# Transfers on POOL's queue tied to an ACT instruction instead of a POOL copy, and fewer of them per step

## The chip, the cores and the metric

The kernel runs on one core of a Trainium2 chip. TensorE (PE) multiplies matrices, VectorE (DVE), ScalarE (ACT) and GpSimd (POOL) work on elements, and SyncE (SP) issues most loads. Each engine takes its instructions from its own queue in order; 16 DMA engines move the data of all queues. The metric is the time of one execution on the device in microseconds (us), the median of the runs shown.

## The reference, cut to what matters

One layer of a hybrid trunk on 512 tokens of width 1024, all in float32:

```
h  = RMSNorm(x);  xa, ga, q, k, v, f, gA, gB = h @ W_in
A  = gelu(ga) * RG_LRU(conv4(xa))         # width 1280, 10 tiles of 128 channels
B  = forgetting_attention(q, k, v, f)     # 16 heads of 64
m  = sigmoid(gA) * (A @ P_A) + sigmoid(gB) * (B @ P_B)
x  = x + RMSNorm(m @ W_out)
u  = conv3(RMSNorm(x) @ W_up);  y = (gelu(u_gate) * u_val) @ W_down
out = x + RMSNorm(y)
```

The last product, by W_down (3072 x 1024), is done with seven half-sized products instead of eight. For that the kernel needs sums of quarters of W_down; four of the seven left factors are such sums.

## The kernel before, in words

**Precision.** Every weight block is split into a rounded part `wh` and the rest `wl`, and each product is three matmuls. A block is 128 partitions by 1024 numbers (512 KB). `Split` loads it on SP (L199); `hi` rounds it on ACT (L205) and `lo` subtracts on DVE (L208). `unit(name)` fetches two blocks ahead of the one that it hands out, so the rounding of a block runs two units before its use.

**Stages, in the order of the trace.** The norm of x with the first four blocks, written out by hand under a manual schedule (L607 to L722); `xa` units t = 4 to 9 (one projection each, L751), with which the gates of tile t - 4 go (`gate_mm`, `gate_act`); four `v` units for tiles t = 10 to 13; four more `v1` units with the decays (`batch`, `inflow`, L809 on); ten `ga` units with scans and output gates (L819 on); sixteen half units of `pa` (L905 on); merge gates; attention, eight pairs of heads (L1128 on); then out, up and down.

**What the gates pass on.** `conv_a(t)` (ACT at L543, DVE at L546) writes `xc[t]`; the pool has six such buffers, so that `conv_a(t)` waits until `xc[t-6]` is no longer read. `gate_act(t)` makes `ix[t]` on ACT (L600) and multiplies it by `xc[t]` on POOL (L601), its last reader. `inflow(t)` takes `ix[t]` on DVE (L790), and the scan (L794) and the output gate (L801, L805) follow.

**The sums of W_down.** `down_sums` yields 48 transfers from DRAM to DRAM, all issued by POOL, each 512 KB: 24 copies (`put`, L160) into tiles `td[0..3][0..5]`, and 24 that add to such a tile (`add`, L163). They come in rounds: in round m four copies, then the additions of rounds m - 1, m - 2 and m - 3. An addition needs the tile that an earlier one wrote. POOL's transfers use eight completion counters in turn, so the ninth waits until the first has landed. The tiles are first read late in the kernel, by the loads of the down product.

**How the transfers get their place.** `background(n, w)` traces a copy of one column of the block `w` on POOL (`tick`, L182), which needs the rounded block, and then n transfers under `tc.issue_after` of that copy. `tc.issue_after(i)` puts the instructions that its block traces on i's own engine behind i in that engine's queue; it adds nothing to instructions of other engines, and it does not wait for i to end. `background` is called once in each of nine `xa`/`v` units (L757), once in each `v1` unit (L813), with two transfers in each `ga` unit (L824) and once in each `pa` half unit (L914).

**Who orders a queue.** Outside the manual regions a planner orders each engine's queue before the program runs. Whenever the engine is free in its plan, it gives it the ready instruction that was traced first; an instruction is ready when everything that it depends on is done in the plan. In a manual region the engine's instructions keep their order among themselves, but instructions traced elsewhere may be put between them. In the plan a transfer of 512 KB holds the queue that issues it for one and the same stretch, copy or addition, a little longer than a load of that size takes alone, whatever goes on in other queues.

Of the kernel before, what the change touches and what calls it, by code (L numbers as in the profile page):

```python
# [8 lines left out]
F32 = mybir.dt.float32  # L9
# [7 lines left out]
P = 128  # L17
# [80 lines left out]
def kernel(  # L98
# [16 lines left out]
    act, dve, pool, pe = nc.scalar, nc.vector, nc.gpsimd, nc.tensor  # L115

    cpool = ctx.enter_context(tc.tile_pool(name="consts", bufs=1))
# [5 lines left out]
    def bank(name):  # L123
        return pspools[-1].tile([P, 512], F32, tag="ps", name=name)
# [32 lines left out]
    def down_sums():  # L157

        def put(t, m, src):
            return lambda: nc.gpsimd.dma_start(td[t][m], src)  # L160

        def add(t, m, src):
            return lambda: nc.gpsimd.dma_start(td[t][m], src, accum_op=ALU.add, max_dma_last_dim=D)  # L163

        for m in range(NS + 3):
            if m < NS:
                for t, (i, c) in enumerate(((0, 0), (1, 1), (0, 1), (1, 0))):
                    yield put(t, m, down_block(i, c, m))
            if 0 <= m - 1 < NS:
                yield add(0, m - 1, down_block(0, 1, m - 1))  # L170
                yield add(2, m - 1, down_block(1, 1, m - 1))
            if 0 <= m - 2 < NS:
                yield add(1, m - 2, td[0][m - 2])
            if 0 <= m - 3 < NS:
                yield add(3, m - 3, td[1][m - 3])

    transfers = down_sums()
    tick = cpool.tile([P, 1], F32, name="tick")

    def background(n, w):  # L180

        i = pool.tensor_copy(out=tick, in_=w[0].bitcast(F32)[:, 0, 0:1])  # L182
        with tc.issue_after(i.ins):
            for _ in range(n):
                next(transfers, lambda: None)()

    class Split:
# [14 lines left out]
            return a if len(self.shape) == 1 else a.rearrange("p (a b) -> p a b", a=self.shape[0])  # L202

        def hi(self):
            act.copy(self.wh, self.raw)  # L205

        def lo(self, engine):
            engine.tensor_tensor(out=self.wl, in0=self.raw, in1=self.wh.bitcast(F32), op=ALU.subtract)  # L208
# [35 lines left out]
    def unit(name, ahead=2):  # L244

        i = where[name]
        fetch(i + ahead)
        return ready.pop(name)
# [6 lines left out]
    def project(dst, unit, ah, al, lo=0, hi=S):  # L255
        wh, wl = unit
        for k in range(KD):
            mm3(dst[:, lo:hi], wh[:, k], wl[:, k], turns(ah[:, k, lo:hi]), turns(al[:, k, lo:hi]), k == 0, k == KD - 1)
# [71 lines left out]
    def v_start(c):  # L330
        for p in range(4 * c, 4 * c + 4):
            vt[p] = vpools[c].tile([P, NT, 4, HD], F32R, tag="vy", name=f"v{p}")
        return [bank(f"v{c}_{t}") for t in range(NT)]
# [197 lines left out]
    with ExitStack() as rg:  # L531
        rt, ixt, tt = {}, {}, {}
        last_act = [None]
        with ExitStack() as r0:
# [22 lines left out]
            def gate_prep(t):  # L557
                n = HROWS[t]
                raw = gwpool.tile([P, 4, P], F32, tag="graw", name=f"graw{t}")
                gh = gwpool.tile([P, 4, P], F32R, tag="gh", name=f"gh{t}")  # L560
                gl = gwpool.tile([P, 4, P], F32R, tag="gl", name=f"gl{t}")
                nc.sync.dma_start(raw, rgw[:, t])
                act.copy(gh, raw)
                stacked = 3 * n <= P
                hw = slice(0, 2 if stacked else 4)
                dve.tensor_tensor(out=gl[:, hw], in0=raw[:, hw], in1=gh[:, hw].bitcast(F32), op=ALU.subtract)
                th = gwpool.tile([P, S], F32R, tag="halo_h", name=f"halo_h{t}")
                tl = None
                if stacked:
                    q = slice(2 * n, 3 * n)  # L570
                    dve.tensor_tensor(out=gh[q, 2:4], in0=raw[q, 2:4], in1=gh[q, 2:4].bitcast(F32), op=ALU.subtract)
                    dsts = ((th, 0, xh), (th, n, xl), (th, 2 * n, xh))
                else:
                    tl = gwpool.tile([P, S], F32R, tag="halo_l", name=f"halo_l{t}", bufs=1)
                    dsts = ((th, 0, xh), (tl, 0, xl))
                for dst, o, src in dsts:
                    for c0, c1 in HALO[t]:
                        i = c0 // P
                        nc.sync.dma_start(dst[o : o + c1 - c0].bitcast(F32), src[i][c0 - i * P : c1 - i * P].bitcast(F32))
                        o += c1 - c0  # L580
                gw[t] = gh, gl, th, tl
# [163 lines left out]
            for t in range(NF, TR + NF):  # L745
                u = unit(order[t][0])
                if t - 3 < TR:
                    gate_prep(t - 3)
                if t < TR:
                    ps = bank(f"xa{t}")  # L750
                    project(ps, u, hh, hl)  # L751
                else:
                    if t == TR:
                        pv = v_start(0)
                    v_mm(t - TR, pv, u)
                if t > NF:
                    background(1, u)  # L757
                pgs = gate_mm(t - NF)
                ga = gate_act(t - NF, pgs)
                if t < TR:  # L760
                    conv_a(t, ps)
                    next(ga)
                    split_a(t)
                else:
                    next(ga)
                next(ga, None)
# [7 lines left out]
        def batch(ops):  # L774
            with tc.issue_after(last_act[0].ins):
                for op in ops:
                    last_act[0] = op()
# [32 lines left out]
        for u in range(4):  # L810
            w = unit(f"v1_{u}")
            v_mm(u, pv, w)
            background(1, w)  # L813
            for t in range(5 * u // 2, 5 * (u + 1) // 2):
                batch([rg_tanh(t), rg_exp(t)])
                inflow(t)
# [3 lines left out]
        for t in range(TR):  # L820
            gas[t] = bank(f"ga{t}")
            w = unit(f"ga{t}")
            project(gas[t], w, hh, hl)
            background(2, w)  # L824
            sq, sc = steps.get(t, ((), ()))
            batch([rg_sqrt(i) for i in sq])
            for i in sc:
                scan(i)
            for i in outs.get(t, ()):
                gate_out(i)  # L830
# [76 lines left out]
        for step, (e, half) in enumerate(PA_ORDER):  # L907
            if half == 0:
                pps[e] = bank(f"pa{e}")
            wh, wl = unit(f"pa{e}_{half}", min(2, len(PA_ORDER) - step))  # L910
            for i in range(5):
                k = 5 * half + i
                mm3(pps[e], wh[:, i], wl[:, i], turns(yh[k], SH), turns(yl[k], SH), k == 0, k == TR - 1)
            background(1, (wh, wl))  # L914
            if half == 1:
                act.copy(pa[:, e], pps[e])
            early_sums(step)
# [28 lines left out]
    def prep_alloc(p):  # L946
        bias = []
        for h in (2 * p, 2 * p + 1):
            B = bpool.tile([P, PO[NT]], F32, tag="B", name=f"B{h}")
            nc.gpsimd.dma_start(B, cnd[h : h + 1, :].partition_broadcast(P))  # L950
            bias.append(B)
        for B in bias:
            for b in (3, 2, 1, 0):
                diag = B[:, PO[b + 1] - P : PO[b + 1]]
                pool.tensor_tensor(out=diag, in0=diag, in1=mask, op=ALU.add)  # L955
        return bias

    pq, pk = held("q0", 1), held("k0", 0)
    with ExitStack() as g2:
# [15 lines left out]
        p, n = gp[0], gp[1]  # L975
# [39 lines left out]
    with ExitStack() as at:  # L1015
# [111 lines left out]
        for p in range(KD):  # L1127
            if p == 0:  # L1128
                pq = held("q1", 1)
            now = scores(p, q, k, bias)  # L1130
            if p < KD - 1:
                bias = prep_alloc(p + 1)
            if 0 < p < KD - 1:
                pq = bank(f"q{p + 1}")
                project(pq, (unit if p > 1 else behind)(f"q{p + 1}"), hh, hl)
            elif p:
                pb_part(0, range(KD - 2))
            if prev is not None:
                pts = pt(p - 1, prev)
            if p < KD - 1:  # L1140
                pk = bank(f"k{p + 1}")
                project(pk, behind(f"k{p + 1}", 2 if p else 0), hh, hl)
                q, k = halves(pq, f"q{p + 1}"), halves(pk, f"k{p + 1}")
            else:
                pb_part(1, range(KD - 3))
            if p == 0:
                b.product(4, b.a[:, Y])
                gate_epilogue(b, "a", 0)
                gate_epilogue(b, "a", 1)
            if prev is not None:  # L1150
                av(p - 1, pts)
            if p == KD - 1:
                pb_part(1, range(KD - 3, KD - 2))
            normalise(now)
            prev = now
        pts = pt(KD - 1, prev)
        i = KD - 2
# [246 lines left out]
    p, n = pairs[NU], pairs[NU + 1]  # L1404
# [381 lines left out]
```

## Time and profile before

| | |
|---|---|
| median of the runs shown (884.02 to 884.9) | 884.7 us |
| the profiled execution | 884.92 us, span 883.1 us |
| PE busy | 868.6 us, 98% of the span |
| DVE, ACT, POOL busy | 743.5, 608.4, 236.3 us |
| DMA, mean over the span | 210 GB/s |

A row of a group names line, engine, operation, what is written from what, the count, then busy us and mean ns, and after the bar the idle time before it and what ended it. A row of a timeline begins with its start and its duration. A row of a DMA queue gives packets, MB, and the time of its packets as a share of 16 engines' time in the window. The row `GB/s` gives the rate in 40 equal slices of the window.

### The profile page before, as it was taken

The numbers are of one execution on the slowest core, as the hardware profiler recorded it, in microseconds if no ns is written. First come the engines' busy times: TensorE is split into PE (matmuls) and PEld (weight loads), VectorE is DVE, ScalarE is ACT, GpSimd is POOL, SyncE is SP. The second block draws the span as 40 slices with busy tenths as digits, with TensorE's granted clock in tenths as the row PEclk, the third lists the DMA queues.
The fourth block names the chain that finished last, engine by engine and source line by source line (L and its number), as shares of the span: only waits on it lengthen the run. The fifth ranks groups of instructions, "written<-read, shape, count | busy, mean of one in ns | idle before, by whom it ended". The sixth has DMA issues, their size and how long they took to land.

```text
span 883.1 us, 15782 instructions
## 1 busy us (share of the span) xinstructions
PE 868.6 (98%) x5856; PEld 792.3 (90%) x5856; DVE 743.5 (84%) x1209; ACT 608.4 (69%) x1031; POOL 236.3 (27%) x283
## 2 busy tenths in 40 slices
PE   9999999999999999999999999999999999999996
PEld 7888888888899998888888889999999999888884
DVE  8986479637978849998868599999999999889997
ACT  7565695532466648776754597888888888688774
POOL 4244344535411024232205100242332332100000
PEclk9999999999999999999999999999999999999999
DMA  7787689999865477453506762879899898699864
GB/s 269 242 288 207 188 214 265 227 273 196 190 148 165 120 261 274 133 173 127 203 26 203 234 200 95 192 178 241 210 222 240 209 233 210 230 384 303 280 192 147
DMA packets 71040, 185.24 MB, mean 210 GB/s; under 512 B 7153, under 2 KB 27681, under 8 KB 70578
## 3 DMA queue, kind: packets, MB, share of 16 engines
q1 hardware_dynamic: 47360, 127.72, 43.4%
q0 software_dynamic: 23456, 56.37, 29.8%
q8 instruction: 46, 0.75, 0.3%
q14 instruction: 32, 0.26, 0.1%
q10 hardware_dynamic: 146, 0.14, 0.0%
HBM read 150.69 MB, written 35.73 MB: 211 GB/s over the span
## 4 chain that ended last, share of the span: by engine, by line
PE 83%; DVE 8%; issue 4%; ACT 2%; POOL 2%; DMA 1%; DVEq 0%; ACTq 0%; POOLq 0%
PE up L464 7%; PE up L462 7%; PE up L461 7%; PE dn L1490 2%; PE dn L1488 2%; PE dn L1489 2%; PE ga L252 2%; PE ga L251 2%; PE ga L253 2%; DVE al L357 2%; PE pb L251 2%; PE xa L251 2%; PE v L341 2%; PE xa L253 2%; PE v L342 2%
## 5 line engine op out<-in xcount | busy, mean ns | idle before, releaser
L397 POOL DMA_DIRECT2D ml<-raw_up x42 | 36.1, 859 | 147.6 <-ACT ml L396 82.5
L1360 DVE SCALAR_TENSOR_TENSOR u<-up,cpt,u 128x511 f32<-128x511 f32 x96 | 71.3, 745 | 3.5 <-ACT u L1354 1.8
L1490 PE MATMUL dn<-wh_dn,al 128*128 128x512 f32 (+1 forms) x180 | 66.6, 370 | 1.3 <-DVE al L357 0.7
L1489 PE MATMUL dn<-wl_dn,ah 128*128 128x512 f32 (+1 forms) x180 | 66.1, 367 | 0.5 <-DVE wl_dn L208 0.5
L1488 PE MATMUL dn<-wh_dn,ah 128*128 128x512 f32 (+1 forms) x180 | 65.8, 366 | 0.2 <-ACT ah L1454 0.2
L461 PE MATMUL up<-sh,th 128*128 128x256 f32 x252 | 59.5, 275 | 0.0
L462 PE MATMUL up<-sl,th 128*128 128x256 f32 x252 | 59.5, 275 | 0.0
L208 DVE TENSOR_TENSOR wl_dn<-raw_dn,wh_dn 128x1024 fp32r<-128x1024 f32 x42 | 52.9, 1259 | 5.4 <-ACT wh_dn L205 5.2
L357 DVE TENSOR_TENSOR tl<-t,th 128x1024 fp32r<-128x1024 f32 x42 | 51.1, 1218 | 0.0
L1354 ACT ACTIVATE u<-up,cpt 128x512 f32<-128x512 f32 x48 | 37.0, 778 | 20.1 <-PE up L464 10.0
L205 ACT CAST wh_dn<-raw_dn 128x1024 fp32r<-128x1024 f32 x42 | 44.4, 1058 | 6.1 <-PE dn L1490 3.7
L461 PEld LDWEIGHTS up<-sh,th 128*128 128x128 f32 x252 | 48.4, 192 | 0.0
L462 PEld LDWEIGHTS up<-sl,th 128*128 128x128 f32 x252 | 48.4, 192 | 0.0
L1368 POOL TENSOR_TENSOR yf<-u,u 128x512 f32<-128x512 f32 x23 | 30.5, 1328 | 59.3 <-issue 46.5
L443 ACT CAST th<-t 128x1024 fp32r<-128x1024 f32 x42 | 43.8, 1044 | 2.4
L1490 PEld LDWEIGHTS dn<-wh_dn,al 128*128 128x128 f32 x180 | 34.1, 189 | 8.0 <-DVE al L357 4.1
L955 POOL TENSOR_TENSOR B<-B,mask 128x128 f32<-128x128 f32 x64 | 30.6, 506 | 34.8 <-DMA B<-cnd 33.7
L461 PE MATMUL up<-h2h,mh 128*128 128x256 f32 x168 | 39.7, 275 | 0.0
L462 PE MATMUL up<-h2l,mh 128*128 128x256 f32 x168 | 39.7, 275 | 0.0
L1489 PEld LDWEIGHTS dn<-wl_dn,ah 128*128 128x128 f32 x180 | 34.1, 189 | 5.8 <-DVE wl_dn L208 1.8
L1050 ACT ACTIVATE P<-P,mx 128x384 f32<-128x384 f32 (+3 forms) x64 | 35.2, 552 | 5.3 <-DVE mx L1045 4.3
L464 PE MATMUL up<-sh,tl 128*128 128x256 f32 x252 | 38.4, 275 | 0.0
(731 smaller groups left out, 3252.4 us busy)
## 6 DMA issues: line engine op xcount, KB each, us to landing
raw_up<-in_w_up_dram SPq DMA_DIRECT2D x48, 512.0 KB, 5.5
td<-in_w_down_dram POOLq DMA_DIRECT2D x36, 512.0 KB, 6.3
raw_dn<-td SPq DMA_DIRECT2D x24, 512.0 KB, 5.4
ml<-raw_up POOLq DMA_DIRECT2D x21, 512.0 KB, 5.4
B<-cnd POOLq DMA_DIRECT2D x16, 640.0 KB, 5.7
raw_dn<-in_w_down_dram SPq DMA_DIRECT2D x18, 512.0 KB, 4.4
raw_wo<-in_w_out_dram SPq DMA_DIRECT2D x16, 512.0 KB, 4.4
td<-td POOLq DMA_DIRECT2D x12, 512.0 KB, 11.2
```

The costliest lines, as they stand in the source:

```text
L205: act.copy(self.wh, self.raw)
L208: engine.tensor_tensor(out=self.wl, in0=self.raw, in1=self.wh.bitcast(F32), op=ALU.subtract)
L251: pe.matmul(dst, ah, bh, start=first, stop=False)
L357: dve.tensor_tensor(out=out, in0=a, in1=b, op=ALU.subtract)
L443: act.copy(self.th[i], self.t[i])
L461: pe.matmul(dst, wh[:, k], turns(ah[:, k]), start=first and k == 0, stop=False, skip_group_check=True)
L462: pe.matmul(dst, wh[:, k], turns(al[:, k]), start=False, stop=False, skip_group_check=True)
L464: pe.matmul(dst, wl[:, k], turns(ah[:, k]), start=False, stop=k == KH - 1, skip_group_check=True)
L1360: dve.scalar_tensor_tensor(out=c[:, s:], in0=ps[:, : S - s], scalar=col(C_CFW + 3 * e + j), in1=c[:, s:], op0=ALU.mult, op1=ALU.add)
L1488: pe.matmul(d[:, x], ah[:, k, tok], bh, start=first, stop=False, skip_group_check=True)
L1489: pe.matmul(d[:, x], ah[:, k, tok], bl, start=False, stop=False, skip_group_check=True)
L1490: pe.matmul(d[:, x], al[:, k, tok], bh, start=False, stop=last, skip_group_check=True)
```

## The change

The `tick` copy is gone. `hi` keeps the last rounding that it traced on ACT in `last_hi`, and `background(n)` traces its transfers under `tc.issue_after` of that ACT instruction. In each `ga` unit one transfer is traced instead of two, in `pa` one in every second half unit, and three at each of the eight pairs of the attention, behind `prep_alloc`. So 31 of the 48 are traced up to the end of `pa`, and the other 17 in the attention.

```
     transfers = down_sums()
-    tick = cpool.tile([P, 1], F32, name="tick")
-    def background(n, w):
-        i = pool.tensor_copy(out=tick, in_=w[0].bitcast(F32)[:, 0, 0:1])
-        with tc.issue_after(i.ins):
+    last_hi = [None]
+    def background(n):
+        with tc.issue_after(last_hi[0].ins):
             for _ in range(n):
                 next(transfers, lambda: None)()
...
         def hi(self):
-            act.copy(self.wh, self.raw)
+            last_hi[0] = act.copy(self.wh, self.raw)
...
                 if t > NF:
-                    background(1, u)
+                    background(1)
...
             v_mm(u, pv, w)
-            background(1, w)
+            background(1)
...
             project(gas[t], w, hh, hl)
-            background(2, w)
+            background(1)
...
-            background(1, (wh, wl))
+            if step % 2:
+                background(1)
...
             if p < KD - 1:
                 bias = prep_alloc(p + 1)
+            background(3)
```

## The prediction

> **What bounds the kernel now.** I read the page first: span, engines, chain.
>
> ```profile
> span 883.1 us, 15782 instructions
> PE 868.6 (98%) x5856; PEld 792.3 (90%) x5856; DVE 743.5 (84%) x1209; ACT 608.4 (69%) x1031; POOL 236.3 (27%) x283
> PE 83%; DVE 8%; issue 4%; ACT 2%; POOL 2%; DMA 1%; DVEq 0%; ACTq 0%; POOLq 0%
> ```
>
> PE sets the time: all its idle time is 14.5 us. So little can be won, and whatever makes PE wait is lost in full. From 24 to 260 us, where the transfers run, the waits of PE are these two:
>
> ```profile
> PE ma L461 <- DVE ma L480: 1.5, 1, 1.5
> PE q L253 <- DVE wl_q L208: 0.9, 1, 0.9
> ```
>
> POOL's groups next: what is removed, what is moved, and what stands beside them.
>
> ```profile
> L182 POOL COPY tick<-wh_pa 128x1 f32<-128x1 f32 x16 | 25.1, 1570 | 24.8 <-ACT wh_pa L205 24.8
> L160 POOL DMA_DIRECT2D td<-in_w_down_dram x24 | 13.3, 556 | 0.5 <-issue 0.5
> L163 POOL DMA_DIRECT2D td<-in_w_down_dram x12 | 12.9, 1180 | 0.0
> L163 POOL DMA_DIRECT2D td<-td x12 | 12.6, 1113 | 10.2 <-DMA td<-td 10.2
> ```
>
> The `tick` copies wait for ACT, and the transfers hardly wait for anything of their own: the tick is what holds them back. The timeline of POOL shows how its queue is ordered.
>
> ```profile
> 11.40 2.39 POOL L208 TENSOR_TENSOR wl_xa<-raw_xa,wh_xa 128x1024 fp32r<-128x1024 f32 x1 [0.76 <-ACT wh_xa L205]
> 19.18 4.75 POOL L208 TENSOR_TENSOR wl_xa<-raw_xa,wh_xa 128x1024 fp32r<-128x1024 f32 x2 [5.39 <-ACT wh_xa L205]
> 24.17 0.18 POOL L182 COPY tick<-wh_xa 128x1 f32<-128x1 f32 x1 [0.24 <-ACT wh_xa L205]
> 24.29 0.72 POOL L160 DMA_DIRECT2D td<-in_w_down_dram  x1
> ...
> 40.10 1.35 POOL L182 COPY tick<-wh_xa 128x1 f32<-128x1 f32 x1
> 40.54 1.32 POOL L160 DMA_DIRECT2D td<-in_w_down_dram  x1
> 46.35 1.28 POOL L601 TENSOR_TENSOR ix<-ix,xc 128x512 f32<-128x512 f32 x1 [4.50 <-ACT ix L600]
> ```
>
> The first ix (L601) is traced in unit t = 4, the transfers before it in units 5 to 8. So the queue is not in the order of the trace: what is ready goes ahead of what is older and not ready.
>
> **The change, part by part.**
>
> 1. *The tie.* The new anchor is an instruction of ACT, the transfers are instructions of POOL, and `issue_after` orders only what is on the anchor's own engine. I therefore expect that no transfer is tied to anything: neither to the rounding nor to its place in `ga`, `pa` or the attention. The copies read an input and write fresh tiles, so the first is ready at the start, and the order above says that they go out whenever POOL's queue is free. That the tie holds in some other way is a rival.
>
> 2. *The ticks removed.* 39 POOL copies (the row above has 16 of them). POOL is 27% busy and nothing on PE's waits names them: 0 us.
>
> 3. *Where the transfers go.* Up to 11 us the rest of POOL's start-up work is ahead. One copy fits before the subtraction at 11.40, some five between it and the one at 19.18, and all others follow from 24 us. By then the first loads have landed, so the start costs about 0 (end: if copies went out from 3 us, they would share the engines with the 4.3 MB of first loads; six copies of 1.5 us, see 4, make up to 9 us). After 24 us the planner books one stretch per transfer, a little over a load's 1.3 us, and puts the older ix in between when ready. The ix are some 7 us apart (10 of them from 46.4 to 107.4 below), so four to five transfers stand between two. Counting from six at 24 us: about 20 before the first ix, 33 before ix of t = 3, 47 before t = 6, and all 48 before t = 7, 8 and 9. Ends: one or two per gap, as today (no effect), and all 48 before the first ix, which I exclude because an older ready ix goes first.
>
> 4. *What they cost on the chip.* The DMA queues in three windows: 0 to 60 us (q0 is POOL's; six copies in it), the rates from 0 to 30 us (loads alone), and 218 to 233 us (additions and loads, the engines full).
>
> ```profile
> q0 software_dynamic: 186, 3.15, 15.0%
> GB/s 0 0 66 289 404 421 388 415 415 415 415 426 415 426 404 415 377 383 377 98 246 360 322 336 101 0 0 0 0 0 169 306 224 126 344 754 175 33 142 350
> q0 software_dynamic: 2072, 2.06, 87.4%
> q1 hardware_dynamic: 614, 1.61, 29.9%
> ```
>
> A copy: 15.0% of 60 us / 6 = 1.5 us of all engines. Loads: 415 GB/s. An addition: in 15 us the loads' 1.61 MB take 3.9 us, which leaves 11.1 us for 2.06 MB, or 3.9 additions of 0.524 MB: 2.8 us each. The planner's equal stretch for both is thus too short for an addition, and it does not count the loads at all. POOL issues a transfer only when the eighth before it has landed, or when the tile that it adds to is there; what stands behind it on POOL waits too. For a full engine set from 2 us on:
>
> - ix of t = 3 stands behind the 33rd transfer, which waits for the 25th: 17 copies and 8 additions, 25.5 + 22.4 = 48 us. Loads until then: some 15 MB (of 19.94 up to 120 us) = 36 us. 2 + 48 + 36 = 86, so this ix ends at about 88 us.
> - The last three ix stand behind the 48th, which waits for the 46th: 24 x 1.5 + 22 x 2.8 = 97.6 us. Loads: 22.96 MB up to 157 us, 55 us, less some that a stalled PE asks for later: 53. 2 + 97.6 + 53 = 152.6; three ix of 1.27 us behind it end at about 155.5 us.
>
> ```profile
> q1 hardware_dynamic: 7584, 19.94, 51.3%
> q1 hardware_dynamic: 8590, 22.96, 44.5%
> L601 POOL TENSOR_TENSOR ix<-ix,xc x10: 1265/1273/1652, 46.4 to 107.4; 128x512 f32<-128x512 f32 x10
> L790 DVE SCALAR_TENSOR_TENSOR ix<-r,ix x10: 684/692/694, 109.9 to 125.3; 128x512 f32<-128x512 f32 x10
> L543 ACT ACTIVATE xc<-xa,cpt x10: 762/777/822, 21.5 to 75.6; 128x512 f32<-128x512 f32 x10
> ```
>
> One rule of the Trainium skill prices this differently: DMA: Bandwidth & Descriptors, "Anatomy of one DMA — SWDGE (gpsimd) path", has about 2 us fixed plus bytes at 436 GB/s, whatever the operation. By it a 512 KB transfer holds the engines 1.2 us, the 46 take 55 us in place of 97.6, and the last ix would end at about 113 us, in time. The measured addition, 2.8 us, speaks against it; the copy's 1.5 us is nearer.
>
> 5. *Who waits for that.* `conv_a(9)` on ACT (last of ten, 75.6 us) needs the buffer that ix of t = 3 frees: ACT stands still until 88 us, and the roundings of the `v` blocks behind it. PE has two units of about 5 to 7 us in hand, so this costs a few us, and not in addition: the next wait ends at a time that the DMA sets. That is `inflow` on DVE.
>
> ```profile
> 120.39 0.68 DVE L790 SCALAR_TENSOR_TENSOR ix<-r,ix 128x512 f32<-128x512 f32 x1
> ...
> 124.16 1.23 DVE L208 TENSOR_TENSOR wl_ga<-raw_ga,wh_ga 128x1024 fp32r<-128x1024 f32 x1 [0.79 <-ACT wh_ga L205]
> 125.30 0.69 DVE L790 SCALAR_TENSOR_TENSOR ix<-r,ix 128x512 f32<-128x512 f32 x1
> ...
> 125.00:160.00 35.00, 35.00 (x164) 30.65 (x163) 33.48 (x53) 22.26 (x43) 13.39 (x20) 1.00 1.04 281
> ...
> 155.62 1.24 DVE L208 TENSOR_TENSOR wl_ga<-raw_ga,wh_ga 128x1024 fp32r<-128x1024 f32 x1
> ...
> L251 PE MATMUL ga<-hh,wh_ga x80: 379/379/379, 126.5 to 177.6; 128*128 128x512 f32 x80
> ```
>
> The last `inflow` moves from 125.3 to 155.5: DVE is 30 us late. Behind it lie the subtractions of the `ga` blocks, the scans and the output gates, and from 125 to 160 us DVE is 33.5 of 35 us busy (third busy time of the row), so it makes nothing up. The `ga` units start every 5.2 us from 126.5: the ninth at 168.1, its subtraction ended at 156.9, so there are 11 us in hand. PE loses 30 - 11 = 19, less 0.7 of DVE's own idle time: **18 us**. At the end of `ga` DVE is less busy and the rest follows unchanged.
>
> 6. *Later stages.* With 17 fewer transfers intended before the attention, or none after 155 us, loads of 185 to 240 us have the engines alone. PE waits 2.4 us in all there, one of the two for DVE's own work: 0, at best -2.
>
> Sum: 0 + 0 + 0 + 18 + 0. The profiled execution took 884.92 us (span 883.1, 1.8 around it), 0.2 above the median: 884.9 + 18 = **903 us**. Its own range: if an addition takes 2.45 or 3.3 us, the 22 make -8 or +11, so 895 to 914; with the loads counted 6 us off either way, 889 to 920.
>
> **The rivals.**
>
> *A: early, but in time.* The transfers float forward, and the ix keep ahead of enough of them (two per gap in place of four or five). Then the last ix comes before 125.3 + 11 = 136 us, nothing reaches PE, and from 185 us on the wait of 0.9 us for `wl_q` and perhaps the 1.5 us end, since loads no longer share with additions: 882.5 to 885. For it: ten ix are released one by one today while additions run. Against it: 97.6 us of transfers and some 50 of loads do not fit before 136. This is the side of not slower; it decides at 136 us.
>
> *A2: additions cost what copies cost.* In one long run the engines take 1.5 us for either: 46 x 1.5 = 69, 2 + 69 + 53 = 124, the last ix at 128 us, before 136: 885. Against it: the 2.8 us above. The rule of the Trainium skill named in 4 would come out here.
>
> *B: the tie holds.* The transfers wait for the roundings, two blocks ahead, and 17 go to the attention, where each wait for a transfer on POOL stands before the next pair's masks. Three additions are 8.4 us of the engines per pair of heads; hidden, or at most 2 us where a mask comes late: 884 to 887. Against it: anchor and transfers are on two engines.
>
> *C: the collision at the start.* Copies ahead of POOL's first subtractions delay x and the first blocks by up to 9 us, and the ix are in time: 885 + 9 = 894.
>
> **How the numbers follow.** My forecast 0.58; A 0.17, A2 0.05, B 0.10, C 0.10. The time is the forecast's, 903. The range 884 to 920 takes in A2, B, C and most of A and leaves out about a tenth at each end. From no change a measurement here tells 0.2%, 1.8 us. Slower: 0.58 + 0.10 + a tenth of A and half of B, some 0.74; same: A2, the other half of B and about half of A, 0.19; faster: 0.07, A's lower end.
>
> **What would show it.** All 48 transfers issued before about 155 us and none in the attention; the first before 24 us; POOL's ix of t = 7 to 9 at about 150 us, behind waits of L163 for a transfer; ACT idle at L543 before 88 us; DVE idle at L790 up to some 25 us, released by POOL; PE idle by about 18 us in `v1` to `ga`. If the transfers run in `pa` and the attention, step 1 is wrong; if ix ends before 136 us, steps 3 or 4 are; if PE is late before 24 us, C is right.

## The result

The changed kernel takes 904.4 us (median; 903.6 to 905.9) beside 884.8 us for the kernel before in the same comparison: a ratio of 1.0228, 95% interval 1.0215 to 1.0241, so 2.3% slower. The forecast was 903 us. Its size holds, and so does the limit that it names. Where PE stands idle, and two terms of the sum, do not.

The profiled execution took 904.1 us. Head of the page, engines and chain of waits, of the changed kernel:

```profile
span 902.3 us, 15700 instructions
PE 874.3 (97%) x5856; PEld 795.7 (88%) x5856; DVE 744.6 (83%) x1209; ACT 610.5 (68%) x1031; POOL 192.0 (21%) x244
PE 69%; DMA 11%; DVE 9%; issue 6%; ACT 3%; POOL 1%; DVEq 0%; ACTq 0%; POOLq 0%
```

The span grew by 19.2 us. PE is idle for 28.0 us in place of 14.5, which is 13.5 of it. The other 5.7 us are in PE's busy time, 874.3 in place of 868.6, although it runs the same 5856 matmuls: some of them ran at a lower clock (below). DMA rose from 1% to 11% of the chain.

The groups of transfers of the changed kernel, by the tile `td` (duration of the instruction on POOL in ns, least, median and most, then first and last start):

```profile
L160 POOL DMA_DIRECT2D td<-in_w_down_dram x24: 486/500/1367, 8.2 to 96.4; - x24
...
L163 POOL DMA_DIRECT2D td<-td x12: 1002/1012/1035, 39.9 to 148.2; - x12
```

The timeline of POOL in the same execution (start, duration):

```profile
90.68 1.01 POOL L163 DMA_DIRECT2D td<-td  x1 [3.78 <-DMA td<-td]
92.08 0.52 POOL L160 DMA_DIRECT2D td<-in_w_down_dram  x1 [0.40 <-DMA td<-in_w_down_dram]
92.62 1.30 POOL L600 TENSOR_TENSOR ix<-ix,xc 128x512 f32<-128x512 f32 x1
...
148.24 1.03 POOL L163 DMA_DIRECT2D td<-td  x1 [4.33 <-DMA td<-td]
148.91 4.11 POOL L600 TENSOR_TENSOR ix<-ix,xc 128x512 f32<-128x512 f32 x3
```

The code moved up one line, so ix is now L600. All 48 transfers are out by 148.2 us, none in the attention. The ix of t = 3 starts at 92.6 us and the last three run from 148.9 to 153.0 us, both behind transfers that waited for an earlier one to land. On DVE the inflows (L789) wait for that, in its timeline:

```profile
150.60 3.58 DVE L789 SCALAR_TENSOR_TENSOR ix<-r,ix 128x512 f32<-128x512 f32 x2 [5.96 <-POOL ix L600]
...
155.24 0.68 DVE L789 SCALAR_TENSOR_TENSOR ix<-r,ix 128x512 f32<-128x512 f32 x1
```

The last inflow starts at 155.2 us, 29.9 later than before. PE, however, had already lost its time elsewhere. Its waits from 30 to 240 us (total, times, longest):

```profile
PE gate L250 <- DMA halo_h<-xh: 8.9, 2, 4.7
PE gate L589 <- DVE xc L545: 3.3, 1, 3.3
PE ga L252 <- DVE wl_ga L207: 1.9, 2, 1.5
PE gate L251 <- DMA halo_l<-xl: 1.8, 2, 1.2
```

Only the third line is DVE's lateness in `ga`. The others are at the gates, in three stalls that end at 43, 71 and 116 us. A `gate` product needs `halo_h` and `halo_l`, rows of neighbouring tiles that small transfers on SP's queue copy (L578), and these came late (the second line is at a matmul that reads a halo too; the profile names DVE, but the matmul's other operand, `gh`, was written at 36.6 us, and the matmul began at 43.0). In the third stall a second cause joins, shown in the waits of ACT from 60 to 200 us:

```profile
ACT xc L542 <- POOL ix L600: 5.9, 1, 5.9
```

That is `conv_a(9)`, which waits for ix of t = 3. The two waits of before in `ma` and `q` are gone.

### The profile page after: what moved, and what is told of

Its sections match the earlier page's. It is cut to its first block, busy times and chain, and to the rows that moved or that the text cites. A ratio compares the mean times of both kernels' runs of the same rounds, so it can differ in the third digit from the quotient of the medians.

```text
span 902.3 us, 15700 instructions
## 1 busy us (share of the span) xinstructions
PE 874.3 (97%) x5856; PEld 795.7 (88%) x5856; DVE 744.6 (83%) x1209; ACT 610.5 (68%) x1031; POOL 192.0 (21%) x244
## 4 chain that ended last, share of the span: by engine, by line
PE 69%; DMA 11%; DVE 9%; issue 6%; ACT 3%; POOL 1%; DVEq 0%; ACTq 0%; POOLq 0%
DMA td<-td 7%; PE up L460 7%; PE up L461 7%; PE up L463 7%; DMA td<-in_w_down_dram 3%; PE dn L1491 2%; PE pa L252 2%; PE pa L251 2%; PE pa L250 2%; PE dn L1490 2%; PE dn L1489 2%; PE q L250 2%; PE pb L250 2%; PE q L252 2%; PE q L251 2%
## 5 line engine op out<-in xcount | busy, mean ns | idle before, releaser
L1489 PEld LDWEIGHTS dn<-wh_dn,ah 128*128 128x128 f32 x180 | 34.1, 189 | 3.9
```

What stands on the lines that cost most here:

```text
L1489: pe.matmul(d[:, x], ah[:, k, tok], bh, start=first, stop=False, skip_group_check=True)
```

## The experiments

The first question is whether the tie does anything, the second whether the gates or the last inflow set the time, the third why the halos are late, the fourth what the additions' price does, the last what a real tie would bring.

### The place in the program does not matter

All calls of `background` in `xa`/`v`, `v1`, `ga` and `pa` are taken out; the attention has eight per pair.

```
-            background(3)
+            background(8)
```

> All 48 transfers are written down in the attention only (eight per pair of heads); the calls in the stages of xa, v, ga and pa are gone, the anchor (ACT's last rounding) stays. Theory, the tie is inert: the transfers float to wherever POOL's queue is free, as in the changed kernel, most of them before 60 us and all before 155 us, and the time is that of the changed kernel, 904 us within 3. Rival, the tie or the place in the program does hold the transfers back: they go out in the attention, after 445 us at the earliest, the first gates are not disturbed, and the time is 882 to 890, or well above 910 if 48 transfers are too many for what is left of the attention.

Measured: 904.3 us, ratio 1.0219 (1.0203 to 1.0234). The transfers go out at the same times, by the tile `td` of this run:

```profile
L160 POOL DMA_DIRECT2D td<-in_w_down_dram x24: 488/502/1372, 9.3 to 96.8; - x24
...
L163 POOL DMA_DIRECT2D td<-td x12: 1005/1014/1037, 40.1 to 147.7; - x12
```

The tie is inert: neither the anchor on ACT nor the place in the program holds a transfer on POOL.

### Less loss at the gates, and the same end

The gates' preparation, with its halo transfers, goes one unit earlier and gets a third buffer.

```
-            gwpool = r0.enter_context(tc.tile_pool(name="rgw", bufs=2, reuse_waits="tile"))
+            gwpool = r0.enter_context(tc.tile_pool(name="rgw", bufs=3, reuse_waits="tile"))
...
+                gate_prep(1)
...
-                if t - 3 < TR:
-                    gate_prep(t - 3)
+                if t - 2 < TR:
+                    gate_prep(t - 2)
```

> The changed kernel with the gates' preparation (their weights and the halo transfers) written one unit earlier, with three buffers in place of two; the 48 early transfers and ix on POOL stay. Theory, two limits lie one behind the other: without late halos PE loses less at the gates, but inflow still waits for the last ix at about 150 us and then costs PE what the gates did not: about 895 to 902. Rival, the late halos alone set the loss and the ix wait comes only because PE was late: 885 to 890.

Measured: 906.4 us, ratio 1.0256 (1.0235 to 1.0277), above both expectations. The same question from another side: the 24 copies under the size limit that the additions have. Their packets came out at 3.7 KB (below), not at 1 KB as the expectations of this and two later runs have it.

```
-            return lambda: nc.gpsimd.dma_start(td[t][m], src)
+            return lambda: nc.gpsimd.dma_start(td[t][m], src, max_dma_last_dim=D)
```

> The changed kernel with the 24 copies cut into packets as small as the additions' (1 KB where they have about 18); bytes, order and places stay. Theory, a halo transfer comes late because its small packets take turns with the copies' large ones on the same engines (the run with plain copies alone, in large packets, had halos landing after up to 24.8 us and lost 33 us): halos land in 5 to 7 us, PE's first two stalls shrink, and the time falls to 893 to 900, where the last ix at about 150 us still holds it. Rival, the sum of bytes decides and not the size of packets: 902 to 907; or small packets make a copy dearer (2.7 us like an addition), the ix come later still, and the time rises above 907.

Measured: 908.1 us, ratio 1.0265 (1.0249 to 1.0281): the last rival's figure, but not for its reason: a copy became hardly dearer (1.4 us, below), and yet the last inflow came 4.2 us later than in the changed kernel. From 8 to 24 us q0 moved 2.63 MB in place of 3.11. From 24 to 150 us it moved as much as in the changed kernel (21.6 MB against 21.5) in 79.3% of the engines' time in place of 77.4%, 2.4 us more. That these two make the 4.2 us is not shown. PE's waits from 30 to 240 us in the run with earlier halos, and its inflows:

```profile
PE ga L252 <- DVE wl_ga L207: 6.2, 3, 3.6
PE gate L589 <- DVE xl L551: 6.0, 1, 6.0
PE gate L250 <- ACT r L597: 3.6, 1, 3.6
PE gate L251 <- DMA halo_l<-xl: 1.8, 1, 1.8
```

```profile
L790 DVE SCALAR_TENSOR_TENSOR ix<-r,ix x10: 677/692/2965, 125.8 to 156.8; 128x512 f32<-128x512 f32 x10
```

The same two views of the run with small packets:

```profile
PE gate L250 <- ACT r L597: 7.1, 1, 7.1
PE ga L252 <- DVE wl_ga L207: 6.6, 3, 4.0
PE gate L251 <- DMA halo_l<-xl: 2.0, 2, 1.4
```

```profile
L789 DVE SCALAR_TENSOR_TENSOR ix<-r,ix x10: 678/691/2968, 127.9 to 159.4; 128x512 f32<-128x512 f32 x10
```

In both, PE comes to `ga` earlier (at 142.4 and 144.5 us, against 147.2 in the changed kernel) and gives it back there: the wait for `wl_ga` grows from 1.9 us to 6.2 and 6.6. What PE saves at the gates, DVE takes in `ga`. Both times are longer than the changed kernel's because the last inflow is 1.6 and 4.2 us later.

### Taking POOL's queue out of the way of ix

The product `ix * xc` goes to DVE; everything else stays.

```
-                pool.tensor_tensor(out=ixt[t], in0=ixt[t], in1=xc[t], op=ALU.mult)
+                dve.tensor_tensor(out=ixt[t], in0=ixt[t], in1=xc[t], op=ALU.mult)
```

> The changed kernel with the ten products ix * xc on DVE in place of POOL; everything else, the 48 early transfers included, stays. It takes away the way from POOL's queue to conv_a and to inflow. Theory 1, what costs the time is ix standing behind transfers in POOL's queue: PE keeps its first two stalls at most in small part, and the time is 884 to 890 (ten products of 1.3 us on DVE, which is about 96% busy there, may take up to 4 back). Theory 2, PE loses at the gates because the halo transfers land late beside full DMA engines, whatever POOL's ix do: the first two stalls (4.2 and about 8 us with the lower clock behind them) stay, less about 3 that the later stages give back, so 893 to 897.

Measured: 893.8 us, ratio 1.0101 (1.0084 to 1.0118), the second theory's figure. PE's waits from 30 to 240 us, and the inflows:

```profile
PE gate L250 <- DMA halo_h<-xh: 5.2, 2, 4.7
PE gate L589 <- DMA halo_h<-xl: 1.3, 1, 1.3
```

```profile
L789 DVE SCALAR_TENSOR_TENSOR ix<-r,ix x10: 684/692/694, 121.8 to 137.4; 128x512 f32<-128x512 f32 x10
```

The wait for `wl_ga` is gone, and so is the third stall, with its wait for ix. The first two stay. Then both edits together, ix on DVE and the gates' preparation one unit earlier:

> Both at once: ix on DVE and the gates' preparation one unit earlier; the 48 early transfers stay. Theory, two limits (ix behind the transfers in POOL's queue, halos behind full engines) and no third: 882 to 887, the waits of PE at the gates gone, and those of before at 185 to 260 us too. Rival, the full engines hurt by more ways (loads of weights that come late for their rounding, the lower clock): 890 or more.

Measured: 892.4 us, ratio 1.0091 (1.0075 to 1.0108): the rival's figure. The edit did not do its part: PE now waits 4.3 us for `halo_l`, which has one buffer only; before the second stall it was issued at 55.0 us, with ix on DVE alone at 57.8, but landed 14.3 us later in place of 11.9. Another 2.7 us go to the gate weights.

Span and last inflow of ten kernels put the two limits side by side (the last three are shown further down; inflow is the last start in the rows of L787 to L790):

| kernel | span | last inflow starts | difference |
|---|---|---|---|
| before | 883.1 | 125.3 | 757.8 |
| changed | 902.3 | 155.2 | 747.1 |
| traced late | 902.5 | 154.7 | 747.8 |
| halos earlier | 904.1 | 156.8 | 747.3 |
| small packets | 906.3 | 159.4 | 746.9 |
| ix on DVE | 891.7 | 137.4 | 754.3 |
| ix on DVE, halos earlier | 890.0 | 136.2 | 753.8 |
| ix on DVE, small packets | 883.3 | 129.0 | 754.3 |
| small copies only | 894.4 | 140.5 | 753.9 |
| plain copies only | 917.0 | 162.6 | 754.4 |

Wherever ix waits in POOL's queue until about 150 us, the end comes 747 us after the last inflow, whatever PE lost before. Where it does not, inflow follows PE, and the distance is 754 (758 before, where the two waits in `ma` and `q` come behind it). So DVE had 7 us in hand behind the last inflow; the changed kernel uses them up. The halos' loss lies underneath, and shows as 9 us at the end when it stands alone.

### Why the halos are late

The first run replaces the additions by plain copies, in the large packets that copies have, and so leaves the sums of W_down out.

```
-            return lambda: nc.gpsimd.dma_start(td[t][m], src, accum_op=ALU.add, max_dma_last_dim=D)
+            return lambda: nc.gpsimd.dma_start(td[t][m], src)
```

> The changed kernel with the 24 additions in memory replaced by plain copies of the same blocks and of the same bytes: the sums of the down weights are left out of what is computed (each tile holds the last block copied to it). It measures what the additions cost beyond a copy. Theory, an addition holds the engines 2.8 us and a copy 1.5: the last ix comes about 22 x 1.3 = 29 us earlier, at some 126 us, before the 136 us from which it costs PE; the stalls at the gates shrink, 885 to 892. Rival, the number of transfers in front of ix on POOL decides and not their price: the ix times and the time stay within 4 us of the changed kernel, 900 to 906.

Measured: 918.1 us, ratio 1.0375 (1.036 to 1.0391). Both theories fail: cheaper transfers made the kernel slower than any other. PE's waits of that run from 30 to 240 us, and its DMA queues from 24 to 60 us (packets, MB, share of 16 engines):

```profile
PE gate L589 <- DMA halo_h<-xl: 19.9, 1, 19.9
PE gate L589 <- DMA halo_h<-xh: 10.8, 1, 10.8
```

```profile
q0 software_dynamic: 542, 8.62, 65.6%
q1 hardware_dynamic: 1399, 3.51, 30.7%
```

POOL's queue q0 moves 8.62 MB in 542 packets, 16 KB each; q1, with loads and halos in packets of 2.5 KB, gets 3.51 MB. That suggests that the two queues take turns by the packet, though a PE that stands still also asks for fewer loads. So the copies' packets alone are changed, in the kernel without the wait for ix, ix on DVE (its edit and that of the small packets, both shown above):

> ix on DVE, and the 24 copies in packets of 1 KB; the 48 early transfers and the halo transfers' places stay. With ix on DVE alone the time was 893.8 and PE still lost 5.2 us and the lower clock behind it to halos. Theory, the copies' large packets make those halos late: the waits for halos shrink to 2 us or less, 886 to 889. Rival, full engines make them late whatever the packets: 892 to 895.

Measured: 884.5 us, ratio 1.0 (0.9989 to 1.0012): the loss is gone, a little further than the theory said. PE's waits from 30 to 240 us in this run:

```profile
PE gate L251 <- DMA halo_l<-xl: 0.9, 1, 0.9
PE gate L589 <- DMA halo_h<-xl: 0.8, 1, 0.8
PE gate L250 <- DMA halo_h<-xh: 0.4, 1, 0.4
```

With ix on DVE alone, the stall of 4.7 us ended at 69.3 us. The transfers to `halo_h` that were issued from 54 to 63 us, in that run and then in this one:

```profile
DMA to landing us min/median/max: 11.3/12.1/12.2
```

```profile
DMA to landing us min/median/max: 7.0/7.7/8.7
```

The engines were as full (q0 had 61.6% of their time from 24 to 60 us, and 65.0% here), and the 48 transfers were not later by much (the last at 153.1 us, and 159.5 here). So large packets, not full engines alone, hold these halos up: between the two runs, 893.8 and 884.5 us, the copies' packets are the one difference. Full engines do delay them too (in the kernel before, such transfers landed after 3.7 to 4.9 us), but here by no more than PE has in hand.

### What the additions' price does

All 48 transfers are made small copies, so that neither the price of an addition nor large packets are left, and the sums of W_down are again left out: the edit of the small packets, and

```
-            return lambda: nc.gpsimd.dma_start(td[t][m], src, accum_op=ALU.add, max_dma_last_dim=D)
+            return lambda: nc.gpsimd.dma_start(td[t][m], src, max_dma_last_dim=D)
```

> The changed kernel with its 24 additions replaced by copies of the same blocks, and all 48 transfers in packets of 1 KB: the sums of the down weights are left out of what is computed. It sets the price of an addition to that of a copy (1.4 to 1.5 us in place of 2.7) without the large packets that made halos late in the run with plain copies. Theory, the price of the additions sets the last ix: it comes at 120 to 130 us in place of 149, no longer holds DVE, and what is left is the loss at the gates, 888 to 895. Rival, the number of transfers ahead of ix in POOL's queue sets it and not what they cost: the last ix stays at 145 us or later, 900 or more.

Measured: 896.1 us, ratio 1.0115 (1.0085 to 1.0145). The products by the tile `ix`:

```profile
L600 POOL TENSOR_TENSOR ix<-ix,xc x10: 1276/1284/1598, 46.6 to 122.2; 128x512 f32<-128x512 f32 x10
```

The last ix starts at 122.2 us in place of about 151: with cheap transfers it is in time, and the number of transfers ahead of it is the same. The theory's mechanism holds; its 895 is exceeded by 1, and PE loses 8.5 us at the gates, in five waits for halos and `wl_xa`, with ix no longer the bound. So packets of 3.7 KB do not always end the loss: here `halo_h` issued from 54 to 63 us landed after 9.8 to 12.2 us, with q0 moving 8.84 MB from 24 to 60 us in place of 5.79 with ix on DVE and small packets. Which of the two, the bytes or the packets (1 KB in an addition), makes that difference was not tried. The price itself stands in the changed kernel's queues from 118 to 148 us, the engines full, nearly all of q0 additions; and that of a small copy in the queues of the run with small packets, from 8 to 24 us, where q0 has copies alone:

```profile
q0 software_dynamic: 4904, 4.87, 101.7%
q1 hardware_dynamic: 556, 2.01, 17.8%
```

```profile
q0 software_dynamic: 714, 2.63, 42.7%
```

The loads' 2.01 MB at 415 GB/s take 4.8 us; 25.2 us remain for 4.87 / 0.524 = 9.3 additions, 2.7 us each. A copy in small packets takes 0.427 x 16 us / 5.0 = 1.4 us. Whether the adding makes an addition dear or its packets of 1 KB (4.87 MB in 4904) stays open.

### A tie that holds, and a faster kernel

The counts of the change with the tick kept, and in the attention an anchor on POOL.

```
-    def background(n, w):
-        i = pool.tensor_copy(out=tick, in_=w[0].bitcast(F32)[:, 0, 0:1])
+    def background(n, w=None):
+        i = pool.tensor_copy(out=tick, in_=w[0].bitcast(F32)[:, 0, 0:1]) if w else last_mask[0]
...
-                pool.tensor_tensor(out=diag, in0=diag, in1=mask, op=ALU.add)
+                last_mask[0] = pool.tensor_tensor(out=diag, in0=diag, in1=mask, op=ALU.add)
...
+                background(3)
```

> The spread of the change with a tie that holds: the tick copy of before stays as anchor in xa, v, ga and pa with the new counts (one per ga, one in every second step of pa), and the three per pair of heads in the attention are anchored on POOL's last addition of a mask. It answers what the change would do if its wait were real. Theory (rival B of the prediction): 17 transfers in the attention are hidden, 884 to 887; if the waits of 0.9 us for wl_q and 1.5 us for ma end because fewer additions run at 185 to 240 us, down to 882.5. Rival: a transfer that waits in front of a mask on POOL delays a pair of heads, above 887, with PE waits in the attention behind POOL.

Measured: 896.3 us, ratio 1.0127 (1.0111 to 1.0142), the rival's side. POOL also issues the loads of the bands `B` of each pair (640 KB). Their landing in the kernel before:

```profile
DMA to landing us min/median/max: 4.2/5.7/8.5
```

Their landing in this run:

```profile
DMA to landing us min/median/max: 4.5/12.0/18.4
```

DVE's wait for their masks in this run, from 320 to 480 us:

```profile
DVE P L1048 <- POOL B L958: 18.0, 10, 4.8
```

Three transfers stand ahead of a pair's bands in the same queue, the bands land 6.3 us later, and DVE waits 18.0 us for masks, where before it waited 1.0. So the counts of the change would cost 11 us even with a tie that works. With fewer per pair they fit: the kernel before, without the calls of the last six half units of `pa`, and with one per pair in the attention (anchor as in the diff above).

```
-            background(1, (wh, wl))
+            if step < 10:
+                background(1, (wh, wl))
...
+                background(1)
```

> The kernel before, with the calls of the second half of pa (ten transfers) moved to the attention, one per pair of heads, tied there to POOL's last addition of a mask; all other calls and the tick stay. Theory: in the run with three per pair the bands that POOL loads (640 KB a pair) landed after 12.0 us in place of 5.7 because they queue behind the transfers; one per pair adds about 2.7 us, inside their slack, and the waits of 1.5 us for ma and 0.9 us for wl_q, which fall where additions fill the engines at 218 to 233 us, end: 882 to 883.5, faster than both kernels. Rival: a pair's bands are late by even one transfer, some 1 to 3 us are lost in the attention: 884 to 888.

Measured: 881.9 us (881.4 to 882.6) beside 884.5, ratio 0.9972 (0.9962 to 0.9982): faster than both kernels. The calls moved are six, not ten as the expectation has it, and five additions then run in the attention. PE has no wait at all between 30 and 240 us; from 218 to 233 us, where before q0 moved 2.06 MB, it moves nothing.

## Why the prediction was right or wrong

**Step 1, the tie inert:** right, shown by the run with all calls in the attention. **Step 2, the ticks at nothing:** not tried alone.

**Step 3, the places:** right. Before ix of t = 0, 3, 6 there were 21, 34 and 47 transfers (20, 33 and 47 forecast), and all 48 before t = 7, 8 and 9. The start cost at most 0.6 us: the first gate begins at 38.9 us, before at 38.3. So C, with its 9 us, is wrong.

**Step 4, the prices:** right in the main. An addition takes 2.7 us (2.8), ix of t = 3 ends at 93.9 us (88), the last at 153.0 (155.5). The sum there has a slip: 152.6 and three ix of 1.27 us make 156.4. The rule of the Trainium skill weighed there, DMA: Bandwidth & Descriptors, "Anatomy of one DMA — SWDGE (gpsimd) path", would have had the last ix at about 113 us, by the estimate made there. The trace does not agree for additions. With small copies alone the last ix ended at 123.5 us, near A2's 128.

**Step 5, who waits:** the binding limit is right, and the last inflow's time too (155.2 against 155.5). Two things in it are wrong. The first is the place of PE's loss. I wrote that the late `conv_a(9)` "costs a few us, and not in addition", and did not look at the halo transfers or at the packets. PE was 20.7 us late when it reached `ga`, and the waits of about 18 us that I expected in `v1` to `ga` came to 1.9. That the loss is not in addition is right, and is why the total holds. The second is the size: 11 us in hand came from the wrong unit. DVE's subtractions for `ga` in the kernel before:

```profile
112.97 1.23 DVE L208 TENSOR_TENSOR wl_ga<-raw_ga,wh_ga 128x1024 fp32r<-128x1024 f32 x1 [0.86 <-ACT wh_ga L205]
119.25 1.23 DVE L208 TENSOR_TENSOR wl_ga<-raw_ga,wh_ga 128x1024 fp32r<-128x1024 f32 x1 [0.79 <-ACT wh_ga L205]
...
131.92 1.22 DVE L208 TENSOR_TENSOR wl_ga<-raw_ga,wh_ga 128x1024 fp32r<-128x1024 f32 x1
136.90 1.20 DVE L208 TENSOR_TENSOR wl_ga<-raw_ga,wh_ga 128x1024 fp32r<-128x1024 f32 x1
142.05 1.22 DVE L208 TENSOR_TENSOR wl_ga<-raw_ga,wh_ga 128x1024 fp32r<-128x1024 f32 x1
148.66 1.22 DVE L208 TENSOR_TENSOR wl_ga<-raw_ga,wh_ga 128x1024 fp32r<-128x1024 f32 x1
```

With the one at 124.16 that the prediction shows these are the first seven, so the one at 155.62 is the eighth, not the ninth. The eighth unit starts at 126.5 + 7 x 5.18 = 162.8 us and needs the result 0.4 later: 6.3 us in hand, not 11. That makes a loss of 29.9 - 6.3 - 0.7 = 22.9; PE entered `pa` 23.1 us late.

**Step 6, later stages:** 0, at best -2, was too little. From 23.1 us late at `pa` PE is 19.2 late at the end: 3.9 us come back. The waits for `ma` and `wl_q` make 2.4 of them; the rest is not traced to a row. The two errors of size nearly cancel (22.9 in place of 18, and 3.9 back in place of 0), so it is partly luck that 903 is so near.

**The rivals.** A and A2 took it that PE loses nothing if ix is in time. The runs with ix in time took 892 to 896, not 882.5 to 885; only ix on DVE with the copies in small packets took 884.5. B had the attention hide 17 transfers, with 884 to 887; its run took 896. All three left out what the transfers do to other transfers.

## What to carry to other kernels

An ordering tie works on the anchor's own engine; test it by moving its calls far away and looking whether anything moves. When two waits of nearly the same length lie on a path, remove each alone and both together, and compare the distance from the suspected event to the end: where that event binds, it is shortest and does not change with what was lost before. Background transfers cost through the small transfers and the queue mates that they hold up, so look at the packet sizes and at the landing times of those before placing them.

## What the runs showed of the hardware that was not expected

**Packets.** Between the run with plain copies and the one with small copies only, the packets of the same 48 copies are the one difference. The queues of the latter from 24 to 60 us:

```profile
q0 software_dynamic: 2430, 8.84, 64.5%
q1 hardware_dynamic: 1991, 5.07, 37.9%
```

POOL's queue moved about as much as with packets of 16 KB (8.62 MB), now in packets of 3.6 KB. The other queue, with packets of 2.5 KB in both, got 37.9% of the engines' time and 5.07 MB, where it had got 30.7% and 3.51 MB; the time fell from 918.1 to 896.1 us. The Trainium skill, DMA: Bandwidth & Descriptors, "Queues, rings and completion order", says that an engine goes round the queues and drains a whole packet before it switches. The two runs agree with that, though a PE that stands still longer, and so asks for fewer loads, may be part of the difference too.

**The clock.** After two of its three stalls PE ran at half its clock. Windows of the changed kernel around its third stall (window; length, then busy us and instructions of PE, PEld, DVE, ACT and POOL; granted clock; DMA share; GB/s):

```profile
112.00:114.00 2.00, 0.10 (x1) 0.13 (x1) 0.00 (x0) 0.00 (x0) 1.00 (x1) 0.71 0.85 336
114.00:116.00 2.00, 0.82 (x2) 0.34 (x3) 0.00 (x0) 0.00 (x0) 1.53 (x2) 0.50 1.05 324
116.00:118.00 2.00, 2.00 (x5) 1.64 (x6) 0.00 (x0) 0.69 (x1) 1.31 (x2) 0.50 1.02 314
118.00:120.00 2.00, 2.00 (x7) 1.58 (x7) 0.00 (x0) 0.36 (x1) 0.47 (x1) 0.58 1.12 298
120.00:122.00 2.00, 2.00 (x11) 1.76 (x10) 0.34 (x2) 0.85 (x3) 0.00 (x0) 1.00 1.23 201
```

The clock falls to 0.50 and is full again after 120 us; the means of the rows make that some 7 us. A stall of 4 to 5 us is thus dearer than its length: in its two stretches at half clock, behind the second and the third stall, PE was busy for 9.7 us, of which by this estimate half, 4.9 us, goes to the clock. That is most of the 5.7 us by which PE's busy time grew. The Trainium skill, TensorE: Matmul & The Clock Gate, "Part 1: The HAM clock gate (the "warmup" mystery)", puts it down to an activity window of about 3.4 us that runs freely, and says that after an idle one the clock is halved. The traces agree that the length of a stall alone does not decide, as with a window that runs freely: the first stall here, 3.3 us long, left the clock at 1.00, and a wait of 2.7 us in the run with ix on DVE and earlier halos took it to 0.50 (the mean from 44 to 46 us). They do not agree that the whole window must be idle: 2.7 us is less than one.
